# A two-layer decoder trunk on one core: Norm's sum one ff1 tile later, two block jobs behind each turned piece, and another chunk order for k's first tile

## The chip, the cores and the metric

The kernel runs on one core of one Trainium2 chip. The metric is the device time of one execution in microseconds. Engines are called as in the profile: PE is TensorE, DVE is VectorE, ACT is ScalarE, POOL is GpSimd, SP is SyncE, which issues most of the DMAs.

## What is computed

A trunk of two layers over 256 tokens and 2048 channels, in fp32. Cut to what matters here:

```
def squared_relu_mlp(h, w1, w2):            # w1: 2048 x 8192, w2: 8192 x 2048
    z = jax.nn.relu(h @ w1)
    return (z * z) @ w2

def reference(x, mem, ...):
    for i in range(2):
        if i == 1:                           # shared keys and values for layer 1
            sk1, sk2, sv = shared_kv(x, ...) # rms_norm(x, kv_norm) @ w_kv, keys normed and rotated
        u = rms_norm(x, mix_norm[i]) @ w_in[i]
        token_out = pooling mixer (layer 0) or differential attention over sk1, sk2, sv (layer 1)
        mem_out = memory_cross_attention(...)
        x = x + jnp.concatenate([token_out, mem_out], axis=-1) @ w_out[i]
        x = x + squared_relu_mlp(rms_norm(x, ffn_norm[i]), w_ff1[i], w_ff2[i])
    return x
```

`rms_norm(x, g)` is `x * rsqrt(mean(x*x) + 1e-6) * g`.

## The kernel before

**Precision and layout.** Activations lie transposed: 16 chunks of 128 channels by 256 tokens (`resid`). Each fp32 operand is split in two parts of a shorter format: `hi`, a cast on ACT (L199 for weights), and `lo`, the rest, a subtraction on DVE (L202 for weights). A product is hi·hi + hi·lo + lo·hi, with fp32 sums in a PSUM bank. An activation chunk holds both parts side by side, 512 columns. In `a_part` (L472, L474) one matmul of 512 columns does hi weights against both halves, and one of 256 columns does lo weights against the high half. In `wide_step` (L506 to L508) the roles are turned: the activation chunk is loaded as weights and four weight blocks are streamed, 512 columns, for two halves `t` of the tokens, so one chunk is six matmuls and a tile has two banks, `ps[0]` and `ps[1]`.

**The feed.** Weights come in blocks of 128 x 128 in the order of their use. `Feed` loads eight blocks per DMA into one of four `raw` buffers, and splits them up to three pieces of work ahead (`AHEAD`) into rings `hi_ring`, `lo_ring` and some spare places (`zb`, `t_acc`, `t_rowsq`). The host lays the weights out in the order that a dry run of the program has written down.

**The order.** The program is written in the order of TensorE's work. `tick()` counts every four blocks; `at(d, fn)` puts a function `d` ticks later. The framework's planner then sets each engine's order from the program order and its own estimates of costs, so that an instruction of one engine may stand ahead of one that the program names earlier.

**The MLP, `ffn(l, ...)`.** ff1 has 64 tiles of 16 blocks (`up_tile`). Tiles 0 to 2 take banks of the tag "mm" (three), tile 3 and all later ones the one bank of the tag "st" (`bank()`, named `x_bank`). ff2 runs beside ff1 in "block jobs": the 8192 inner channels are taken in 32 pairs of chunks, and a pair's 2 x 2 blocks are multiplied with seven products instead of eight, with sums and differences of weight slabs (DVE L240, L254, and an accumulating DMA from POOL, L163) and of activations (`convert`, DVE L831 to L836, cast L841, low half L845). A slab is four jobs of 6, 3, 6 and 6 matmuls (`product`, L916, L918, L919, into seven banks `p`). There are 60 slabs, 240 jobs. `tiles_at(s)` gives each slab a due time in tiles, and `due(tiles, least)` runs jobs up to that time, at least `least` of them, while more than 12 are left; it is called ahead of each tile with `least=2` and inside it after 4, 8 and 12 blocks. The last 12 jobs run in `down`.

**Norm's sum.** The MLP's input norm is put off: `fx` has the gain but not the factor. `rstd_from("x")` multiplies the running sum of squares `acc` (POOL, L745 and L746 in `add_square`, one pair for each output chunk of the layer before) with ones on TensorE (L531, into a bank of the tag "st" by `stat()`), and turns it into 1/sqrt with three ACT operations (L421, L423, L425) and two on DVE (L368, called from `stt`). It is called in `up_tile` behind tile 0; three ticks later `columns` does the same per token (L540), six ticks later the factor is squared on ACT (L862).

**Turned pieces.** Towards the end of ff1 the left half of ff2's output is complete in token-major rows. `close_left` takes it from the banks, and four pieces are transposed on TensorE (`turn_left`, L1020, into `bank()`, copied out by ACT, L816) ahead of tiles 60 to 63 and added to `resid` on DVE (L1028).

**The end of the MLP and k's first tile.** `down` runs eight down tiles for what is left of ff2 (tiles 0 to 2 in `x_bank`, tiles 3 to 7 in "mm" banks, emptied by DVE L891, added L892) and transposes the other eight chunks (`finish_banks`, L1059, L1060) at ticks between them. Each closed chunk goes into `x_kv` (ACT L450, DVE L368). Then `map_tile` for the keys takes the 16 chunks of `x_kv` as `wide_step`s, into banks of `pair_of_banks`:

```
def pair_of_banks(c, name):
    if c % 2:
        return [pp.tile([P, 512], F32, tag="s", bufs=2, name=name) for _ in range(2)]
    return [mmt(name) for _ in range(2)]     # two of the three "mm" banks
```

Of the kernel before, what the change touches and what calls it, by code (L numbers as in the profile page):

```python
# [19 lines left out]
NK = 16  # L20
# [310 lines left out]
def program(ctx, tc, plan, dry, xT, memT, par, lam, cst, wst, yT):  # L331
    nc = tc.nc
# [15 lines left out]
    def at(d, fn, rank=1):  # L348
        pend.setdefault(now[0] + d, []).append((rank, fn))

    def tick():
        now[0] += 1
        for _, fn in sorted(pend.pop(now[0], []), key=lambda x: x[0]):
            fn()
# [103 lines left out]
    def a_part(ps, w, l, n, ks, xs, first=True, last=True, between=None):  # L458


        ks = list(ks)
        i = 0
        while i < len(ks):
            if between:
                between(i)
            two = []
            for k in ks[i : i + 2 - feed.pos % 2]:
                two.append((i, k % NK, *feed.block((w, l, k, n, 1))))
                feed.used()
                i += 1  # L470
            for c, k, hi, lo in two:
                nc.tensor.matmul(ps, hi, xs[:, k, :], start=first and c == 0, stop=False)  # L472
            for c, k, hi, lo in two:
                nc.tensor.matmul(  # L474
                    ps[:, T : 2 * T], lo, xs[:, k, 0:T], start=False,
                    stop=last and c == len(ks) - 1,
                )
            if feed.pos % 4 == 0:
                tick()
# [10 lines left out]
            if feed.pos % 4 == 0:  # L490
                tick()

    def wide_step(ps, what, xs, k):
        hi, lo = feed.quad(what)
        x = [(xs[:, k, t * P : t * P + P], xs[:, k, T + t * P : T + t * P + P]) for t in range(2)]
        if what[:2] == ("w_mem_kv", 0) and k < 2:

            for t in range(2):
                nc.tensor.matmul(ps[t], x[t][0], hi, start=k == 0, stop=False)
            for t in range(2):  # L500
                nc.tensor.matmul(ps[t], x[t][1], hi, start=False, stop=False)
            for t in range(2):
                nc.tensor.matmul(ps[t], x[t][0], lo, start=False, stop=False)
        else:
            for t in range(2):
                nc.tensor.matmul(ps[t], x[t][1], hi, start=k == 0, stop=False)  # L506
                nc.tensor.matmul(ps[t], x[t][0], hi, start=False, stop=False)  # L507
                nc.tensor.matmul(ps[t], x[t][0], lo, start=False, stop=k == NK - 1)  # L508
        feed.used(4)
        tick()  # L510

# [1 line left out]
        for k in range(NK):  # L513
            wide_step(ps, (w, l, k, c, 4), xs, k)

    def map_tile(ps, w, l, blocks, xs):

        for k in range(NK):
            wide_step(ps, [(w, l, k, n, 1) for n in blocks], xs, k)

    def by_head(row, d):

# [6 lines left out]
    def rstd_from(name):  # L529
        st = stat("st_" + name)  # L530
        nc.tensor.matmul(st, ones_d, acc[name], start=True, stop=True)  # L531
        r = cp.tile([P, T], F32, tag="r_" + name, name="r_" + name)
        rsqrt(r, st)
        return r

    def columns(name, tag="st"):

        st = pp.tile([P, T], F32, tag=tag, bufs=1, name="tc_" + name)
        for i in range(2):
            nc.tensor.matmul(  # L540
                st[:, 2 * i : 2 * i + 2], acc[name][:, i * P : i * P + P], ones_d[:, 0:2],
                start=True, stop=True,
            )
        v = tp.tile([P, 2], F32, tag="m2", bufs=12, name="cv")
        nc.vector.tensor_scalar_add(v, st[:, 0:4].rearrange("p (a b) -> p a b", b=2)[:, :, 0], EPS)
        col = cp.tile([P, 2], F32, tag="c_" + name, name="c_" + name)
        rsqrt_cols(col, v)
        col2 = cp.tile([P, 2], F32, tag="d_" + name, name="d_" + name)
        nc.vector.tensor_mul(col2, col, col)
        return col, col2  # L550
# [218 lines left out]
    def ffn(l, xs, tags, done):  # L769
# [52 lines left out]
        def convert(i):  # L822
            u = staged[:, i % 2, :]
            n = 512 if i == 31 else 1024 if i >= 28 else 896

            def block(b, c=1):
                return u[:, b * P : (b + c) * P]

            def combine():
                twice = block(A21).unsqueeze(1).to_broadcast([P, 2, P])  # L830
                nc.vector.tensor_add(  # L831
                    block(S1, 2).rearrange("p (a c) -> p a c", a=2), twice,
                    block(A22, 2).rearrange("p (a c) -> p a c", a=2),
                )
                nc.vector.tensor_add(block(S2), block(S1), block(A11))
                nc.vector.tensor_add(block(S4), block(A12), block(S2))  # L836
                at(1, lambda: when(lambda: i == 31 or pair_free[i % 5], high))

            def high(a=0, b=n):
                pair_free[i % 5] = False  # L840
                nc.scalar.copy(pair(i)[:, 0, a:b], u[:, a:b])  # L841
                at(1, lambda: low(a, b))

            def low(a, b):
                nc.vector.tensor_sub(  # L845
                    pair(i)[:, 1, a:b], u[:, a:b], pair(i)[:, 0, a:b].bitcast(F32)
                )
                if a == 0:
                    done_pairs.add(i)

            if i < 31:
                return combine()
            assert pair_free[i % 5]
            high(512, 1024)
            at(1, combine)

        def up_tile(i, ps, between=None):
            a_part(ps, "w_ff1", l, i, range(NK), xs, between=between)
            if i == 0:
                r.append(rstd_from("x"))  # L860
                at(3, lambda: r.append(columns("x", "o")[1]))
                at(6, lambda: nc.scalar.activation(r[0], r[0], AF.Square))  # L862
            out = nc.scalar.copy(two_y[:, 1 - i % 2, :], ps)
            if i == 3 and not dry:
                feed.cast_behind = [out.ins.name] * 3
            if i % 2 == 0:
                return
            left, right = two_y[:, :, 0:T], two_y[:, :, T : 2 * T]
            d = 0 if i == 63 else 1

            def add():
                nc.vector.tensor_add(left, left, right)

            at(1, add) if d else add()

            def square():
                assert i < 4 or i // 2 - 2 in done_pairs
                nc.scalar.activation(left, left, AF.Relu)
                u = staged[:, i // 2 % 2, 512:1024].rearrange("p (a c) -> p a c", a=2)
                nc.scalar.activation(u, left, AF.Square)  # L880
                at(1, lambda: convert(i // 2))

            at(1 + d, square)
# [207 lines left out]
        def tiles_at(s):  # L1091

            return early[s] if s < 12 else 20 + (s - 12) * 44 / 46

        def due(tiles, least=0):
            n = 0
            while len(jobs) > 12:
                s, j = jobs[0]
                if tiles_at(s) + j * (tiles_at(s + 1) - tiles_at(s)) / 4 > tiles and n >= least:
                    break  # L1100
                one_job()
                n += 1
# [6 lines left out]
        for i in range(4, 64):  # L1109
            due(i, 2)  # L1110
            if turns:
                turn_left(turns.pop(0))
                due(i, 1)
            up_tile(i, bank(), lambda b, i=i: due(i + b / 16) if b > 0 and b % 4 == 0 else None)
        due(64)
        assert len(jobs) == 12 and not turns
# [30 lines left out]
    xs = sp.tile([P, NK, 512], F32R, tag="S2", name="xs0")  # L1147
# [61 lines left out]
    for i in range(2):  # L1209
        c = slice(2 * i, 2 * i + 2)  # L1210
# [21 lines left out]
    ps = [mmt("mq0"), pp.tile([P, 512], F32, tag="o", bufs=1, name="mq0")]  # L1232
# [12 lines left out]
    for i in range(2):  # L1245
        c = slice(2 * i, 2 * i + 2)
# [110 lines left out]
    x_kv = sp.tile([P, NK, 512], F32R, tag="S2", name="x_kv")  # L1357
# [42 lines left out]
    at(14, lambda: c1.extend(columns("x")))  # L1400
    for c in range(3):
        ps = pair_of_banks(c, "k1")
        map_tile(ps, "w_kv", 0, (2 * c, 2 * c + 1, 6 + 2 * c, 7 + 2 * c), x_kv)
        rows = key_rows(ps, c1, 64)
        rope(rows, ktab)
        for i in range(2):
            at(
                9,
                lambda i=i, c=c, rows=rows: turn_rows(
                    rows, 2 * i, kT[:, 4 * c + 2 * i : 4 * c + 2 * i + 2, :], gcol(G_KN)  # L1410
                ),
            )
    for c in range(3):
        ps = pair_of_banks(c + 1, "v1")
# [8 lines left out]
    ps = pair_of_banks(0, "mk1")  # L1423
    b_tile(ps, "w_mem_kv", 1, 0, mems1)
    mrow1 = key_rows(ps, mem_c, P)
    ps = pair_of_banks(1, "mv1")
# [7 lines left out]
    for t in range(2):  # L1434
        four = "p (h d) -> p h d"
        hi, v4 = mv1[:, t, :].rearrange(four, h=4), ps[t].rearrange(four, h=4)
        split_rows(hi, mv1_lo[:, :, t, :], v4, mem_c[0][:, t : t + 1])
    for i in range(2):
        c = slice(2 * i, 2 * i + 2)
# [114 lines left out]
    for c in range(3):  # L1554
        ps = pair_of_banks(0, "q1")
# [17 lines left out]
    for h in range(4):  # L1573
        ps = mmt("mq1")
        x = ps[:, 0:T]
        if h < 3:
            a_part(ps, "w_in", 1, 12 + h, range(NK), x_mx)
            x = vt("mq_x")
# [102 lines left out]
```

## Time and profile before

| | us |
|---|---|
| median of 3 runs | 2009.33 (2009.01 to 2012.25) |
| profiled execution | 2008.67 |
| its span, first to last instruction | 2006.9 |
| TensorE busy | 1992.0 (99%) |
| VectorE busy | 1731.0 (86%) |
| ScalarE busy | 1456.1 (73%) |
| GpSimd busy | 156.8 (8%) |

The span is what the trace covers; the profiled execution's time is 1.77 us longer. The mean granted clock of TensorE is 0.999 of full speed, and the DMA engines read 418.00 MB, 209 GB/s over the span. A row of the timeline reads: start in us from the span's start, duration in us, engine, line of the kernel, operation, output <- inputs, shapes, how many are merged, and in brackets the idle time before it and what ended it. In such a row of PE with `x2` the duration runs to the end of the second matmul; matmuls overlap, so the distance of their starts is the pace.

### The profile page before, as it was taken

Reading aid. Unit: us, or ns where it says so; the run is one execution under the profiler, and the core shown is the slowest. Engines: PE = TensorE matmul, PEld = TensorE weight load, DVE = VectorE, ACT = ScalarE, POOL = GpSimd, SP = SyncE. Lnnn points to the kernel's source line nnn. Section 1 sums busy time; section 2 is a strip of 40 time slices with the busy share of each in tenths; the row PEclk is TensorE's granted clock in tenths of the full one; section 3 lists DMA queues with packets and bytes.
Section 4 is the critical chain, followed back from the end, with each engine's and each line's share of the span. In section 5 each row is a group of like instructions: output and inputs, shape, how many; then the busy total and the mean of one; then the engine's idle time right before and its main releaser. Section 6 shows DMA issues by size and latency. Waiting matters only on the chain.

```text
span 2006.9 us, 30220 instructions
## 1 busy us (share of the span) xinstructions
PE 1992.0 (99%) x10510; PEld 1700.8 (85%) x10510; DVE 1731.0 (86%) x2574; ACT 1456.1 (73%) x2316; POOL 156.8 (8%) x187
## 2 busy tenths in 40 slices
PE   9999999999999999999999999999999999999998
PEld 8888888888888888888888888888888888888887
DVE  8888778989989899999765698868889999899998
ACT  7765567687786878877665699557777777868875
POOL 0001210000000001000000000320000010000000
PEclk9999999999999999999999999999999999999999
DMA  9555577777778777755565533667777777777773
GB/s 318 173 190 192 183 226 217 226 221 235 226 229 240 222 223 232 225 178 168 181 235 193 179 127 127 201 204 221 225 218 233 229 235 230 222 238 222 231 227 114
DMA packets 145018, 422.09 MB, mean 210 GB/s; under 512 B 16353, under 2 KB 19041, under 8 KB 144865
## 3 DMA queue, kind: packets, MB, share of 16 engines
q1 hardware_dynamic: 127440, 388.69, 58.5%
q0 software_dynamic: 17280, 31.46, 9.3%
q8 instruction: 82, 1.34, 0.3%
q14 instruction: 72, 0.58, 0.1%
q10 hardware_dynamic: 144, 0.01, 0.0%
HBM read 418.00 MB, written 2.10 MB: 209 GB/s over the span
## 4 chain that ended last, share of the span: by engine, by line
PE 97%; DVE 2%; ACT 1%; POOL 0%; issue 0%; ACTq 0%; DVEq 0%
PE x_bank L472 23%; PE x_bank L474 11%; PE p L919 9%; PE p L916 9%; PE p L918 9%; PE wo L472 6%; PE wo L474 3%; PE u L472 2%; PE u L474 1%; PE q L506 1%; PE k L506 1%; PE k L508 1%; PE q L508 1%; PE k L507 1%; PE q L507 1%; PE v L506 1%
## 5 line engine op out<-in xcount | busy, mean ns | idle before, releaser
L202 DVE TENSOR_TENSOR lo_ring<-raw,hi_ring 128x512 fp32r<-128x512 f32 (+1 forms) x632 | 545.1, 870 | 114.9 <-ACT hi_ring L199 106.7
L199 ACT CAST hi_ring<-raw 128x512 fp32r<-128x512 f32 (+1 forms) x632 | 474.8, 756 | 232.5 <-DVE lo_ring L202 57.4
L472 PE MATMUL x_bank<-fx,hi_ring 128*128 128x512 f32 x1440 | 451.0, 394 | 0.8 <-ACT room L816 0.7
L202 DVE TENSOR_TENSOR lo_ring<-slab,hi_ring 128x1024 fp32r<-128x1024 f32 x229 | 279.3, 1223 | 64.8 <-ACT hi_ring L199 63.9
L199 ACT CAST hi_ring<-slab 128x1024 fp32r<-128x1024 f32 x229 | 240.2, 1052 | 128.1 <-PE x_bank L472 62.4
L474 PEld LDWEIGHTS x_bank<-fx,lo_ring 128*128 128x128 f32 x1440 | 270.3, 188 | 62.3 <-DVE lo_ring L202 1.6
L474 PE MATMUL x_bank<-fx,lo_ring 128*128 128x256 f32 x1440 | 283.9, 278 | 0.0
L472 PEld LDWEIGHTS x_bank<-fx,hi_ring 128*128 128x128 f32 x1440 | 236.8, 189 | 21.1 <-ACT room L816 1.7
L163 POOL DMA_DIRECT2D room<-in_w x120 | 103.7, 864 | 1143.1 <-DMA room<-in_w 1117.4
L916 PE MATMUL p<-hi_ring,z 128*128 128x512 f32 x446 | 174.7, 392 | 0.0
L918 PE MATMUL p<-hi_ring,z 128*128 128x512 f32 x446 | 174.4, 391 | 0.0
L919 PE MATMUL p<-lo_ring,z 128*128 128x512 f32 x446 | 172.8, 390 | 0.1
L472 PE MATMUL wo<-cat,hi_ring 128*128 128x512 f32 x512 | 161.9, 397 | 0.3 <-DVE rc L443 0.3
L472 PE MATMUL x_bank<-fx,zb 128*128 128x512 f32 x512 | 160.3, 395 | 0.7 <-ACT room L816 0.7
L474 PEld LDWEIGHTS x_bank<-fx,zb 128*128 128x128 f32 x512 | 96.1, 188 | 22.1 <-DVE zb L202 0.4
L474 PEld LDWEIGHTS wo<-cat,lo_ring 128*128 128x128 f32 x512 | 96.0, 188 | 21.9
L202 DVE TENSOR_TENSOR zb<-slab,zb 128x1024 fp32r<-128x1024 f32 x71 | 86.8, 1223 | 24.3 <-ACT zb L199 24.1
L199 ACT CAST zb<-slab 128x1024 fp32r<-128x1024 f32 x71 | 74.8, 1054 | 39.9 <-PE x_bank L472 23.1
L474 PE MATMUL wo<-cat,lo_ring 128*128 128x256 f32 x512 | 101.6, 279 | 0.0
L474 PE MATMUL x_bank<-fx,zb 128*128 128x256 f32 x512 | 101.0, 278 | 0.0
L919 PEld LDWEIGHTS p<-lo_ring,z 128*128 128x128 f32 x446 | 83.7, 188 | 18.6 <-DVE lo_ring L202 0.5
L916 PEld LDWEIGHTS p<-hi_ring,z 128*128 128x128 f32 x446 | 83.7, 188 | 12.0
(435 smaller groups left out, 4242.9 us busy)
## 6 DMA issues: line engine op xcount, KB each, us to landing
raw<-in_w SPq DMA_DIRECT2D x484, 512.0 KB, 4.1
slab<-in_w SPq DMA_DIRECT2D x120, 512.0 KB, 5.5
room<-in_w SPq DMA_DIRECT2D x180, 256.0 KB, 3.4
room<-in_w POOLq DMA_DIRECT2D x120, 256.0 KB, 6.2
slab<-in_w SPq DMA_DIRECT2D x60, 256.0 KB, 4.8
memraw<-in_mem SPq DMA_DIRECT2D x5, 512.0 KB, 4.4
resid<-in_x SPq DMA_DIRECT2D x8, 256.0 KB, 5.9
out_y<-resid SPq DMA_DIRECT2D x16, 128.0 KB, 1.9
```

What stands on the lines that cost most here:

```text
L163: self.nc.gpsimd.dma_start(self.t1[i], right, accum_op=ALU.add)
L199: self.last_cast = self.nc.scalar.copy(hi, src)
L202: low = self.nc.vector.tensor_sub(lo, src, hi.bitcast(F32))
L472: nc.tensor.matmul(ps, hi, xs[:, k, :], start=first and c == 0, stop=False)
L474: nc.tensor.matmul(ps[:, T : 2 * T], lo, xs[:, k, 0:T], start=False, stop=last and c == len(ks) - 1,)
L506: nc.tensor.matmul(ps[t], x[t][1], hi, start=k == 0, stop=False)
L507: nc.tensor.matmul(ps[t], x[t][0], hi, start=False, stop=False)
L508: nc.tensor.matmul(ps[t], x[t][0], lo, start=False, stop=k == NK - 1)
L916: nc.tensor.matmul(ps, a[1], hi, start=new, stop=False, **again)
L918: nc.tensor.matmul(ps, a[0], hi, start=False, stop=False, **again)
L919: nc.tensor.matmul(ps, a[0], lo, start=False, stop=end, **again)
```

## The change

Three edits. (1) Norm's sum, with the two steps timed from it, is called behind tile 1 of ff1 instead of tile 0, in both layers. (2) Behind each turned piece `due` is called with `least=2` instead of 1. (3) In k's first tile (c = 0) the chunks of `x_kv` are taken in the order 0 to 5, 8 to 11, 6, 12 to 15, 7, and `wide_step` takes its first and last step from that list. The host's layout of the weights follows, since it is written in the order of use; the other two tiles of k keep their order.

```
         def up_tile(i, ps, between=None):
             a_part(ps, "w_ff1", l, i, range(NK), xs, between=between)
-            if i == 0:
+            if i == 1:
                 r.append(rstd_from("x"))
                 at(3, lambda: r.append(columns("x", "o")[1]))
                 at(6, lambda: nc.scalar.activation(r[0], r[0], AF.Square))
...
             if turns:
                 turn_left(turns.pop(0))
-                due(i, 1)
+                due(i, 2)
...
-    def wide_step(ps, what, xs, k):
+    def wide_step(ps, what, xs, k, ks=range(NK)):
...
-                nc.tensor.matmul(ps[t], x[t][1], hi, start=k == 0, stop=False)
+                nc.tensor.matmul(ps[t], x[t][1], hi, start=k == ks[0], stop=False)
...
-                nc.tensor.matmul(ps[t], x[t][0], lo, start=False, stop=k == NK - 1)
+                nc.tensor.matmul(ps[t], x[t][0], lo, start=False, stop=k == ks[-1])
...
-    def map_tile(ps, w, l, blocks, xs):
+    def map_tile(ps, w, l, blocks, xs, ks=range(NK)):
 
-        for k in range(NK):
-            wide_step(ps, [(w, l, k, n, 1) for n in blocks], xs, k)
+        for k in ks:
+            wide_step(ps, [(w, l, k, n, 1) for n in blocks], xs, k, ks)
...
-        map_tile(ps, "w_kv", 0, (2 * c, 2 * c + 1, 6 + 2 * c, 7 + 2 * c), x_kv)
+        ready = [0, 1, 2, 3, 4, 5, 8, 9, 10, 11, 6, 12, 13, 14, 15, 7] if c == 0 else range(NK)
+        map_tile(ps, "w_kv", 0, (2 * c, 2 * c + 1, 6 + 2 * c, 7 + 2 * c), x_kv, ready)
```

## The prediction

> **What bounds the kernel now.** I read the page first, then TensorE's own waits, then the timeline round each wait on TensorE, VectorE, ScalarE and GpSimd, and last the windows for the granted clock.
>
> ```profile
> span 2006.9 us, 30220 instructions
> PE 1992.0 (99%) x10510; PEld 1700.8 (85%) x10510; DVE 1731.0 (86%) x2574; ACT 1456.1 (73%) x2316; POOL 156.8 (8%) x187
> PE 97%; DVE 2%; ACT 1%; POOL 0%; issue 0%; ACTq 0%; DVEq 0%
> ```
>
> TensorE is busy 1992.0 of 2006.9 us and the chain that ended last is TensorE for 97%. The change takes no matmul away, so all that it can win lies in the 14.9 us between busy time and span, and in time at a lower clock. TensorE's waits name nearly all of it:
>
> ```profile
> PE st_x L531 <- POOL acc L746: 4.1, 2, 2.1
> PE k L506 <- DVE room L891: 2.9, 1, 2.9
> PE x_bank L472 <- ACT room L816: 1.4, 2, 0.7
> ```
>
> Columns: total us, times, longest. Each part of the change stands opposite one of these rows: Norm's sum, k's first tile, the turned piece. Together 8.4 us. The question for each is whether the edit removes what the wait waits for.
>
> The pace and the granted clock (eighth column) come from three windows, the first two behind k's wait, the third behind Norm's sum in layer 1:
>
> ```profile
> 930.40:934.00 3.60, 3.58 (x9) 2.88 (x10) 3.27 (x8) 1.83 (x4) 0.00 (x0) 0.54 0.30 90
> 934.00:938.00 4.00, 4.00 (x18) 3.28 (x18) 4.00 (x9) 3.42 (x10) 0.00 (x0) 0.98 0.58 183
> 1335.00:1339.00 4.00, 3.83 (x21) 3.35 (x22) 0.00 (x0) 2.34 (x4) 0.68 (x2) 1.00 1.00 292
> ```
>
> At full clock 18 matmuls of 512 columns start in 4.00 us, 0.22 us each; a block job or a chunk of k, six of them, is 1.33 us.
>
> **Part 1, Norm's sum behind the second ff1 tile.** Layer 0, TensorE, GpSimd, then VectorE:
>
> ```profile
> 256.35 0.39 PE L474 MATMUL ff<-fx,lo_ring 128*128 128x256 f32 x2
> 258.76 0.70 PE L531 MATMUL st_x<-acc,ones_d 128*128 128x256 f32 x2 [2.02 <-POOL acc L746]
> 259.11 0.81 PE L472 MATMUL ff<-fx,hi_ring 128*128 128x512 f32 x2
> 263.48 0.50 PE L540 MATMUL tc_x<-ones_d,acc 128*128 128x2 f32 x4
> 265.32 0.63 PE L472 MATMUL ff<-fx,hi_ring 128*128 128x512 f32 x2
> 270.89 0.63 PE L472 MATMUL x_bank<-fx,hi_ring 128*128 128x512 f32 x2
> 276.46 0.40 PE L916 MATMUL p<-hi_ring,z 128*128 128x512 f32 x1
> ```
>
> ```profile
> 257.11 1.59 POOL L746 TENSOR_TENSOR acc<-acc,psq 128x256 f32<-128x256 f32 x1
> ```
>
> ```profile
> 263.46 0.69 DVE L240 TENSOR_TENSOR slab<-room,slab 128x512 f32<-128x512 f32 x1 [5.33 <-DMA room<-in_w]
> 264.07 0.42 DVE L368 SCALAR_TENSOR_TENSOR rs_t<-st_x,rs_t 128x256 f32<-128x256 f32 x1
> 264.52 0.43 DVE L368 SCALAR_TENSOR_TENSOR r_x<-rs_t,rs_h 128x256 f32<-128x256 f32 x1
> 271.97 1.09 DVE L845 TENSOR_TENSOR z<-stage,z 128x896 fp32r<-128x896 f32 x1
> 274.11 0.69 DVE L202 TENSOR_TENSOR t_rowsq<-room,t_acc 128x512 fp32r<-128x512 f32 x1
> ```
>
> The sum's matmul stands behind the first ff1 tile and needs the last square, which GpSimd ends at 257.11 + 1.59 = 258.70. The tile had issued all it had by about 256.58 (the two 256-column matmuls of the row 256.35 at half of 0.22 us each). One tile lasts 270.89 - 265.32 = 5.57 us, so behind the second tile the sum comes up at about 256.58 + 5.57 = 262.15, 3.4 us after the square is done. The wait is covered. Price of the removal in layer 0: 258.76 - 256.58 = 2.18 us, and some 0.1 us because the restart is slow (0.81 us for the first two matmuls, where the same two take 0.63, is partly that). Layer 1:
>
> ```profile
> 1332.68 0.40 PE L474 MATMUL ff<-fx,lo_ring 128*128 128x256 f32 x2
> 1335.16 0.70 PE L531 MATMUL st_x<-acc,ones_d 128*128 128x256 f32 x2 [2.09 <-POOL acc L746]
> 1352.87 0.40 PE L916 MATMUL p<-hi_ring,z 128*128 128x512 f32 x1
> ```
>
> ```profile
> 1350.34 0.69 DVE L202 TENSOR_TENSOR t_rowsq<-room,t_acc 128x512 fp32r<-128x512 f32 x1
> ```
>
> There 1335.16 - 1332.90 = 2.26 us and the same 0.1. Sum: 4.4 + 0.2 = 4.6 us. The sum's own matmuls are only moved.
>
> What is late next? Three ScalarE operations and two of VectorE (rows 264.07 and 264.52) now come one tile later, the two columns of sums at the third quarter of the third tile, and the square of r_x in the fourth. No DMA and no GpSimd instruction is issued by the moved step, and no order on SP or GpSimd changes by it. VectorE stands at row 263.46 waiting for a transfer. That transfer is not timed by the tiles, so it lands at the same time while TensorE is 2.2 us earlier. From there VectorE has work in its queue to 274.80 (274.11 + 0.69); the first block job, 276.46 now, would start at 274.2. It needs the z low half, done at 271.97 + 1.09 = 273.06: 1.1 us in hand. Job 1 needs the row at 274.11 at its third matmul, 1.33 + 0.44 us after job 0 starts, at 276.0: 1.2 us in hand. Layer 1 is alike: that row ends at 1351.03, 1.84 us ahead of its first job where layer 0 has 1.66. Bound: nothing lost, or up to the 2.2 us of each layer if the rows slide. I take 0.2 us in all.
>
> The fourth tile takes the only bank of the sum (`bank()` and `stat()` share tag "st"). Until now two tiles lay between, now one: from 262.6 to the fourth tile at about 262.6 + 5.57 + 0.36 = 268.5, where 0.36 is what the row 263.48 delays the next matmuls (they start at 263.84). The last reader of the sum is the row 264.07; it follows the row 263.46, over at 264.15, and at worst two low halves that would stand ready there, some 1.2 us each: about 267.0. 1.5 us in hand; cost nothing. Part 1: 4.6 - 0.2 = 4.4 us won.
>
> **Part 2, two jobs behind a turned piece.** Where do the two waits stand? Both at the fourth piece:
>
> ```profile
> 879.63 0.60 PE L1020 MATMUL x_bank<-const,room 128*128 128x128 f32 x4
> 880.27 0.58 ACT L816 COPY room<-x_bank 128x512 f32<-128x512 f32 x1 [0.93 <-PE x_bank L1020]
> 880.90 0.73 PE L472 MATMUL x_bank<-fx,zb 128*128 128x512 f32 x2 [0.68 <-ACT room L816]
> ```
>
> No p matmul stands between piece and tile. The code says why. `due` stops at 12 jobs left, whatever `least` is, and 240 jobs less 12 end with job 3 of slab 56. Tile 60 takes jobs 53.3, 54.0, piece, 54.1; tile 61 takes 54.3, 55.0, piece, 55.1; tile 62 takes 55.3, 56.0, piece, 56.1, and 56.2 within the tile; tile 63 takes 56.3, piece, and nothing is left. After the change 54.2, 55.2 and 56.2 stand behind the first three pieces instead of behind block 12 of the tile, and tile 63 is as before. So the 1.4 us stay. At the first three pieces the one job covers the copy already; piece 0 of layer 0:
>
> ```profile
> 849.07 0.58 ACT L816 COPY room<-x_bank 128x512 f32<-128x512 f32 x1
> 849.75 0.69 PE L472 MATMUL x_bank<-fx,zb 128*128 128x512 f32 x2
> 850.27 1.23 DVE L202 TENSOR_TENSOR lo_ring<-slab,hi_ring 128x1024 fp32r<-128x1024 f32 x1
> ```
>
> The copy is over at 849.65 and the tile starts at 849.75 with no wait. The moved jobs cost their 1.33 us of matmuls in either place. Risk: their low halves must be there about 4 us earlier. 54.2 would ask for its low half two matmuls behind where the tile starts now, at 850.2, and has it at 850.27 + 1.23 = 851.5 in the old order: at worst 1.3 us, at six pieces 8 us. But the change also brings its preparation ahead of the tile's, and the tile's first weights are ready to stand between. I take 0, with 0 to 2.4 us (0.4 at each) for the range.
>
> **Part 3, k's chunks.** TensorE and VectorE at k's start:
>
> ```profile
> 926.03 0.40 PE L506 MATMUL k<-hi_ring,x_kv 128*128 128x512 f32 x1
> 927.07 0.40 PE L507 MATMUL k<-hi_ring,x_kv 128*128 128x512 f32 x1
> 930.42 0.56 PE L506 MATMUL k<-hi_ring,x_kv 128*128 128x512 f32 x1 [2.95 <-DVE room L891]
> ```
>
> ```profile
> 928.36 1.67 DVE L368 SCALAR_TENSOR_TENSOR x_kv<-resid,param,x_kv 128x256 fp32r<-128x256 f32 x4
> 929.95 0.42 DVE L891 TENSOR_TENSOR room<-ff,r_x 128x256 f32<-128x256 f32 x1
> 934.56 0.48 DVE L368 SCALAR_TENSOR_TENSOR x_kv<-resid,param,x_kv 128x256 fp32r<-128x256 f32 x1
> ```
>
> The wait comes after five matmuls, within the first two chunks, and ends with L891: that line empties a bank of a down tile and writes no chunk. Down tiles 3 to 7 turn through the three "mm" banks, so k's two banks are those of tiles 5 and 6. The rows of L891 stand in the order of the tiles; this one is tile 6, held up by the four x_kv splits at 928.36. It is the bank for k's second half of the rows. Both orders begin with chunks 0 to 5, so the change leaves this wait where it is. Chunk 7, the last to close, is there at 935.04; the old order asks for it seven chunks of 1.33 us after 926.03 at the earliest, 935.3, and in fact after the wait and the slow stretch. So the new order has nothing to win behind the wait either: 0, between 0 and the whole 2.95 us. The Trainium skill, "TensorE: Matmul & The Clock Gate", Part 2, states that matmuls stay in program order and only weight loads are pulled ahead; by that k's ready chunks cannot step in for the late bank, and the trace agrees, with nothing issued between 927.07 and 930.42. A reordering queue would have made it 2.95 us less.
>
> The wait has a second price. In 930.40 to 934.00 the granted clock is 0.54 and 9 matmuls take what 18 take in the next 4.00 us: 3.6 - 2.0 = 1.6 us. The idle times of 2.02 and 2.09 us at Norm's sum left the clock at 1.00. So it falls for an idle time of some 3 us, perhaps only if it lies so. k starts 2.3 us earlier after the change, and the 1.6 us may not come back. The Trainium skill, same page, Part 1, states a free-running window of 3413 ns, of which one idle one halves the clock; the trace agrees as far as the slow stretch is about that long, and by that rule the 1.6 us would go or stay by chance.
>
> **Sum.** Profiled execution 2008.67 us (span 2006.9 and 1.77 outside it). Part 1 -4.4, part 2 0, part 3 0: 2004.3 us. The median of the runs, 2009.33, is 0.66 above the profiled one; from it the sum is 2004.9. A measurement of this kernel can tell about 0.2%, 4.0 us: faster is below 2005.3, slower above 2013.4. The forecast lies just beyond the edge.
>
> **Rivals.**
> A, forecast: part 1 alone works, 2004.3 (2003.3 to 2005.6). Chance 0.41.
> B: the same, and the slow stretch behind k's wait does not return: 2004.3 - 1.6 = 2002.7. For it: the lower idle times cost no clock. Against: the 2.95 us stay as they are. 0.25.
> C: the diff does all that it says; k's wait and its slow stretch go too, 2004.3 - 2.95 - 1.6 = 1999.8, with the piece's wait 1998.4. Against: the bank, and the job count. 0.08.
> D: the covers are too thin. VectorE, late by its transfer, holds the first block job, or a low half holds the jobs behind the pieces; 1.0 to 3.5 us come back: 2006.5. For it: VectorE has only 1.1 us in hand. 0.18.
> E, slower: the sum's bank. If the row 264.07 falls in VectorE's queue behind everything that stands there till 274.80, the fourth tile waits from 268.5 to about 275.2, 6.7 us, and such an idle time brings the slow clock with 1.6: 8.3 in each layer, 16.6 - 4.6 = 12 us lost, 2020.7. It costs more than it wins from a read that ends 2.3 us late, behind 270.8. Against: until now the row came right behind the transfer. 0.08.
>
> From these: faster 0.62 (A mostly, B, C), same 0.30 (the rest of A, D), slower 0.08. The range 2001.0 to 2007.8 holds A, B and most of D; C and E lie outside.
>
> **What would show it.** Right: no wait of st_x for acc; the sum's matmul about 5.6 us later than the first tile's end; the x_bank waits for L816 still two of 0.7 us behind the fourth piece; k still waiting about 3 us for L891. Wrong: a wait of x_bank for rs_t or r_x at the fourth tile, of p for z or lo_ring at the first block job or behind a piece, or k's wait gone.

## The result and the profile after

The changed kernel takes 2003.36 us (median of 7 runs, 2001.65 to 2004.7); the kernel before, timed beside it, 2009.33 us (median of 7 runs, 2008.37 to 2012.53). The ratio is 0.9968, with a 95% interval of 0.9956 to 0.9979: 6.0 us, or 0.3%, faster. The profiled execution took 2003.26 us, 5.41 us less than the one of before.

The page of the kernel after: its span, busy times and the shares of the chain that ended last.

```profile
span 2001.5 us, 30206 instructions
PE 1990.5 (99%) x10510; PEld 1699.4 (85%) x10510; DVE 1730.7 (86%) x2574; ACT 1456.2 (73%) x2316; POOL 157.7 (8%) x187
PE 97%; DVE 1%; ACT 1%; issue 0%; DMA 0%; SPq 0%; DVEq 0%; ACTq 0%
```

The span is 5.4 us shorter and TensorE's busy time only 1.5 us: most of what went was idle time. Which idle time it was, TensorE's waits tell (total us, times, longest), from the longest down:

```profile
PE k L506 <- DVE room L891: 2.9, 1, 2.9
PE x_bank L472 <- ACT room L816: 1.4, 2, 0.7
PE warm L413 <- PEq L1655: 0.8, 1, 0.8
PE mk L499 <- DVE mems L1173: 0.7, 1, 0.7
```

The wait of st_x for acc, 4.1 us before, is gone. The first three rows are those of before, to the tenth. The fourth is not in the kernel before, but it lies in the first 9 us, and the loop behind it (mk, L506) starts at 11.1 us in both kernels: it cost nothing. TensorE's timeline at Norm's sum, layer 0, and the fourth tile and first block job of layer 1:

```profile
261.88 0.39 PE L474 MATMUL ff<-fx,lo_ring 128*128 128x256 f32 x2
262.11 0.59 PE L531 MATMUL st_x<-acc,ones_d 128*128 128x256 f32 x2
262.35 0.82 PE L472 MATMUL ff<-fx,hi_ring 128*128 128x512 f32 x2
266.72 0.50 PE L540 MATMUL tc_x<-ones_d,acc 128*128 128x2 f32 x4
268.56 0.63 PE L472 MATMUL x_bank<-fx,hi_ring 128*128 128x512 f32 x2
274.13 0.40 PE L916 MATMUL p<-hi_ring,z 128*128 128x512 f32 x1
...
1342.39 0.63 PE L472 MATMUL x_bank<-fx,hi_ring 128*128 128x512 f32 x2
1347.96 0.40 PE L916 MATMUL p<-hi_ring,z 128*128 128x512 f32 x1
```

No row has a bracket with an idle time. The first block job starts at 274.13 (276.46 before, 2.33 us earlier), in layer 1 at 1347.96 (1352.87 before, 4.91 us earlier). VectorE beside it:

```profile
262.07 0.69 DVE L240 TENSOR_TENSOR slab<-room,slab 128x512 f32<-128x512 f32 x1 [4.00 <-DMA room<-in_w]
266.72 0.43 DVE L368 SCALAR_TENSOR_TENSOR rs_t<-st_x,rs_t 128x256 f32<-128x256 f32 x1 [1.08 <-ACT rs_t L425]
271.59 1.08 DVE L845 TENSOR_TENSOR z<-stage,z 128x896 fp32r<-128x896 f32 x1
```

The sum's bank is read out at 266.72 + 0.43 = 267.15, 1.41 us ahead of the fourth tile; the z low half is done at 271.59 + 1.08 = 272.67, 1.46 us ahead of the first job. TensorE at the first and the fourth turned piece:

```profile
846.00 0.60 PE L1020 MATMUL x_bank<-const,room 128*128 128x128 f32 x4
848.07 0.63 PE L472 MATMUL x_bank<-fx,zb 128*128 128x512 f32 x2
848.53 0.62 PE L919 MATMUL p<-lo_ring,z 128*128 128x512 f32 x2
...
877.21 0.60 PE L1020 MATMUL x_bank<-const,room 128*128 128x128 f32 x4
878.48 0.73 PE L472 MATMUL x_bank<-fx,hi_ring 128*128 128x512 f32 x2 [0.68 <-ACT room L816]
```

Behind the first piece the second job now runs, and the planner's order has the tile's first two matmuls ahead of the two that need the job's low half, with no wait. Behind the fourth piece nothing has changed. TensorE and VectorE at k:

```profile
923.40 0.43 PE L506 MATMUL k<-hi_ring,x_kv 128*128 128x512 f32 x1
924.50 0.39 PE L507 MATMUL k<-hi_ring,x_kv 128*128 128x512 f32 x1
927.83 0.50 PE L506 MATMUL k<-hi_ring,x_kv 128*128 128x512 f32 x1 [2.95 <-DVE room L891]
...
925.78 1.66 DVE L368 SCALAR_TENSOR_TENSOR x_kv<-resid,param,x_kv 128x256 fp32r<-128x256 f32 x4
927.37 0.41 DVE L891 TENSOR_TENSOR room<-ff,r_x 128x256 f32<-128x256 f32 x1
```

k starts 2.63 us earlier, waits in the same place for the same line, and behind it stands the same slow stretch (windows; the eighth column is the granted clock):

```profile
929.00:932.50 3.50, 3.50 (x10) 2.73 (x9) 3.43 (x9) 2.12 (x6) 0.00 (x0) 0.51 0.48 150
932.50:936.00 3.50, 3.50 (x17) 2.90 (x16) 3.50 (x8) 3.50 (x9) 0.00 (x0) 1.00 0.72 219
```

### The profile page after: what moved, and what is told of

Same layout as the page of the kernel before. It is cut to its first block, busy times and chain, and to the rows that moved or that the text cites. A ratio compares the mean times of both kernels' runs of the same rounds, so it can differ in the third digit from the quotient of the medians.

```text
span 2001.5 us, 30206 instructions
## 1 busy us (share of the span) xinstructions
PE 1990.5 (99%) x10510; PEld 1699.4 (85%) x10510; DVE 1730.7 (86%) x2574; ACT 1456.2 (73%) x2316; POOL 157.7 (8%) x187
## 4 chain that ended last, share of the span: by engine, by line
PE 97%; DVE 1%; ACT 1%; issue 0%; DMA 0%; SPq 0%; DVEq 0%; ACTq 0%
PE x_bank L472 23%; PE x_bank L474 11%; PE p L919 9%; PE p L916 9%; PE p L918 9%; PE wo L472 6%; PE wo L474 3%; PE u L472 2%; PE ff L472 1%; PE u L474 1%; PE q L506 1%; PE k L506 1%; PE k L508 1%; PE q L508 1%; PE k L507 1%; PE v L508 1%
## 5 line engine op out<-in xcount | busy, mean ns | idle before, releaser
L202 DVE TENSOR_TENSOR lo_ring<-raw,hi_ring 128x512 fp32r<-128x512 f32 (+1 forms) x631 | 542.9, 868 | 113.4 <-ACT hi_ring L199 104.7
L472 PE MATMUL x_bank<-fx,hi_ring 128*128 128x512 f32 x1424 | 445.8, 394 | 1.4 <-ACT room L816 1.4
L202 DVE TENSOR_TENSOR lo_ring<-slab,hi_ring 128x1024 fp32r<-128x1024 f32 x222 | 270.3, 1221 | 64.4 <-ACT hi_ring L199 63.8
L199 ACT CAST hi_ring<-slab 128x1024 fp32r<-128x1024 f32 x222 | 232.6, 1052 | 125.7 <-PE x_bank L472 58.6
L472 PE MATMUL x_bank<-fx,zb 128*128 128x512 f32 x528 | 165.0, 394 | 0.0
L474 PEld LDWEIGHTS x_bank<-fx,zb 128*128 128x128 f32 x528 | 99.2, 188 | 22.4
L202 DVE TENSOR_TENSOR zb<-slab,zb 128x1024 fp32r<-128x1024 f32 x78 | 95.1, 1219 | 24.0 <-ACT zb L199 23.6
L199 ACT CAST zb<-slab 128x1024 fp32r<-128x1024 f32 x78 | 82.2, 1053 | 41.2 <-PE x_bank L472 27.8
L472 PEld LDWEIGHTS x_bank<-fx,zb 128*128 128x128 f32 x528 | 87.5, 189 | 7.5
```

Source lines behind the costliest of these rows:

```text
L199: self.last_cast = self.nc.scalar.copy(hi, src)
L202: low = self.nc.vector.tensor_sub(lo, src, hi.bitcast(F32))
L474: nc.tensor.matmul(ps[:, T : 2 * T], lo, xs[:, k, 0:T], start=False, stop=last and c == len(ks) - 1,)
```

## The experiments

Theory ahead of the runs: the move of Norm's sum is the whole gain; the other two parts move work that waits for nothing they touch. Rivals: the jobs or the chunk order bring a share of their own, or k's wait hangs on something other than the bank.

**One part at a time.** The kernel before with the sum's move alone, `e1_norm`:

```
-            if i == 0:
+            if i == 1:
                 rstd_from("x")
```

> The kernel before with Norm's sum moved alone. My theory (only this part works): 4.6 us faster than before, about 2003.9 against 2008.67 in a profiled execution, and the same as the whole change within 0.8 us; the two waits of st_x for acc are gone, k's wait of 2.9 us and the two of 0.7 us at x_bank stay. Rival (the other two parts bring the 0.8 us by which the whole change went beyond 4.6): 0.8 us or more slower than the whole change.

Measured: 2003.92 us (6 runs) against 2010.57 (22 runs of the kernel before), ratio 0.9968 (0.9957 to 0.998), the ratio of the whole change. (That the two medians are so near is in part the clock, as the table below shows.) The k and piece waits stand at 2.9 and 1.4 us as ever. One thing is new: in layer 1 the fourth tile waits for the sum's bank. VectorE and ScalarE, then TensorE:

```profile
1339.31 0.69 DVE L240 TENSOR_TENSOR slab<-room,slab 128x512 f32<-128x512 f32 x1 [6.59 <-DMA room<-in_w]
1342.19 0.68 DVE L872 TENSOR_TENSOR room<-room 128x512 f32<-128x512 f32 x1
1342.91 0.63 ACT L878 ACTIVATE room<-room 128x512 f32<-128x512 f32 x1 [3.77 <-DVE room L872]
1343.45 0.40 ACT L425 ACTIVATE rs_t<-rs_h 128x256 f32<-128x256 f32 x1
1343.96 0.42 DVE L368 SCALAR_TENSOR_TENSOR rs_t<-st_x,rs_t 128x256 f32<-128x256 f32 x1 [1.08 <-ACT rs_t L425]
...
1344.44 0.73 PE L472 MATMUL x_bank<-fx,hi_ring 128*128 128x512 f32 x2 [0.45 <-DVE rs_t L368]
```

This is the wait that rival E names, at 0.45 us instead of 6.7. The way to it leads over ScalarE: the last of the sum's three operations there (L425) stands behind L878, L878 waits for VectorE's L872, and L872 stands in VectorE's queue behind L240 and two low halves. From the start of L240 to that of rs_t it is 4.65 us here and in both layers of the whole change. In this execution the transfer that L240 waits for landed about 2 us later against the sum's matmul than in the profiled execution of the whole change. So the 1.4 us in hand there can be used up by one late transfer.

The second job alone, `e2_jobs`:

```
-                due(i, 1)
+                due(i, 2)
```

> The kernel before with two block jobs behind each turned piece alone. My theory: no change, 0 +- 0.5 us against before, since no job is left behind the fourth piece where the two waits of 0.7 us are; both waits stay. Rival 1 (the diff's aim): both gone, 1.4 us faster. Rival 2 (the moved jobs want their low halves too early): waits of p for lo_ring or zb behind the first three pieces, up to 0.4 us each, 2.4 us slower.

The chunk order alone, with the list in `wide_step` as in the change, `e3_order`:

```
-        map_tile(ps, "w_kv", 0, (2 * c, 2 * c + 1, 6 + 2 * c, 7 + 2 * c), x_kv)
+        ready = [0, 1, 2, 3, 4, 5, 8, 9, 10, 11, 6, 12, 13, 14, 15, 7] if c == 0 else range(NK)
+        map_tile(ps, "w_kv", 0, (2 * c, 2 * c + 1, 6 + 2 * c, 7 + 2 * c), x_kv, ready)
```

> The kernel before with the new chunk order of k's first tile alone. My theory: 0 +- 0.5 us, since k's wait is for a bank; the wait of k L506 for DVE L891 stays at 2.9 us and the half clock behind it too. Rival (the wait is for the chunks that close last): the wait gone, 2.9 to 4.5 us faster.

Measured: `e2_jobs` 2009.43 us (11 runs), ratio 0.9996 (0.9987 to 1.0005); `e3_order` 2010.01 us (11 runs), ratio 0.9997 (0.9988 to 1.0006). By their medians, neither can be told from no change. Both profiles show the three waits of before at their old sizes, to 0.1 us, and no new one where the change touches anything.

The timelines tell the two apart, in stretches that hold no slow clock. From layer 0's first block job to k's start it is 649.57 us in before, 649.54 in `e1_norm`, 649.73 in `e3_order`; with the second job 649.28 in `e2_jobs` and 649.27 in after. From the end of VectorE's last operation to the end of the span, where the last outputs are written, it is 3.6 to 3.7 us in those three and 3.2 in these two; in layer 1, from the first job to the last matmul, the five lie within 0.1 us of each other. So the second job does bring something, about 0.3 + 0.4 to 0.5 us, some 0.8 in all. The 0.3 us lie between the fourth turned piece and k, not at the two waits; why a gain comes there and in the last outputs, no run shows.

What these two profiles also show is the clock. Windows behind Norm's sum in `e2_jobs` (both layers), then the same window as the first in the kernel before, then the window behind k's wait in `e3_order`:

```profile
259.50:262.90 3.40, 3.40 (x11) 2.85 (x11) 0.00 (x0) 1.90 (x4) 0.00 (x0) 0.50 1.02 267
1338.10:1341.50 3.40, 3.40 (x13) 2.92 (x12) 0.00 (x0) 2.04 (x4) 0.89 (x1) 0.50 0.97 289
```

```profile
259.50:262.90 3.40, 3.40 (x21) 2.97 (x20) 0.00 (x0) 2.35 (x4) 0.89 (x1) 1.00 0.99 274
```

```profile
930.40:934.00 3.60, 3.47 (x15) 2.84 (x16) 3.53 (x9) 2.59 (x6) 0.00 (x0) 1.00 0.21 71
```

The idle time ahead of the sum in `e2_jobs` is 2.0 us, as before, and here it is followed by 3.4 us at clock 0.50, 11 matmuls where the other execution had 21. In `e3_order` k waited its 2.95 us and lost nothing behind it. Whether an idle time of 2 or 3 us is followed by half clock thus differs from execution to execution of what is the same code there. The spread of the runs goes with the clock; sorted by their mean granted clock, mean us (runs):

| kernel | 1.000 | 0.999 | 0.998 | 0.997 |
|---|---|---|---|---|
| before | | 2008.95 (11) | 2010.47 (26) | 2012.14 (10) |
| after | 2001.65 (1) | 2003.43 (4) | 2004.65 (2) | |
| e1_norm | 2003.12 (3) | 2005.07 (2) | 2005.94 (1) | |
| e2_jobs | | 2008.53 (4) | 2009.96 (5) | 2011.50 (2) |
| e3_order | 2007.54 (1) | 2009.01 (4) | 2010.23 (3) | 2012.59 (3) |
| e4_banks | 2002.68 (4) | 2003.36 (1) | | |
| e5_turns | 2002.39 (2) | 2003.49 (2) | 2004.22 (1) | |
| e6_fourth | | 2001.96 (3) | 2002.99 (2) | |
| e7_third | | 2011.07 (2) | 2012.09 (4) | 2013.00 (5) |
| e8_all | 2000.98 (2) | 2002.77 (3) | | |
| e9_spread | | 2000.91 (5) | | |
| e10_square | | 2003.91 (4) | 2005.22 (2) | |

A thousandth of mean clock is about 1.5 us; one stretch of 3.4 us at half clock is 1.7/2007, or 0.85 thousandths. A stretch can also be twice as long. Behind k's wait in `e1_norm`:

```profile
927.30:934.10 6.80, 6.04 (x14) 4.79 (x15) 6.24 (x14) 2.83 (x6) 0.00 (x0) 0.50 0.30 96
```

At equal clock (0.999) after is 5.5 us faster than before, and `e1_norm` 1.3 to 1.6 us slower than after (three columns). Against the runs of before that were timed beside them, `e1_norm` is 4.2 to 4.6 us faster at equal clock and `e2_jobs` 0.6 to 1.0. A column is as wide as 1.5 us and holds few runs, so this is weak by itself; it agrees with the timelines in giving the second job part of the gain.

**The sum one tile later still,** `e7_third`, the change with the sum behind the third tile:

```
-            if i == 1:
+            if i == 2:
```

> The changed kernel with Norm's sum behind the third ff1 tile instead of the second. Nothing is left out. Theory (the fourth tile takes the sum's only bank, so the move has a far end): the fourth tile waits for rs_t, the sum's last reader on VectorE, 2 to 4 us in each layer, 4 to 8 us slower than the whole change and more where the clock falls. Rival (the tile's bank is no bound): same as the whole change within 0.5 us.

Measured: 2012.36 us (11 runs) against 2010.36 (15), ratio 1.001 (1.0001 to 1.0019): the gain is gone and 2 us with it. The wait stands elsewhere than expected. TensorE, then VectorE:

```profile
271.19 0.50 PE L916 MATMUL p<-hi_ring,z 128*128 128x512 f32 x1 [2.13 <-DVE z L845]
272.94 0.68 PE L472 MATMUL x_bank<-fx,hi_ring 128*128 128x512 f32 x2
...
270.05 1.09 DVE L845 TENSOR_TENSOR z<-stage,z 128x896 fp32r<-128x896 f32 x1
272.41 0.42 DVE L368 SCALAR_TENSOR_TENSOR rs_t<-st_x,rs_t 128x256 f32<-128x256 f32 x1
```

With the sum later in the only bank, the planner put the first block jobs ahead of the fourth tile. These then wait for z, 4.7 us in both layers together, which the fourth tile had covered. A tile of distance from the sum to the fourth tile is needed; the second tile is the last place that keeps it.

**What made the sum late,** `e10_square`, the kernel before with the sum in its old place, but the last chunk's square on ScalarE and its addition on VectorE instead of GpSimd:

```
         if act:
             nc.scalar.activation(sq, src, AF.Square)
+            nc.vector.tensor_add(acc[key], acc[key], sq)
+            return
...
-            add_square("x", resid[:, n, :], n == 0)
+            add_square("x", resid[:, n, :], n == 0, n == NK - 1)
```

> The kernel before, with Norm's sum left behind the first ff1 tile, but the last chunk's square taken by ScalarE and added by VectorE instead of both on GpSimd. Nothing is left out. Theory (the sum waited for GpSimd's queue, where a DMA's issue of 1 us and two slow operations of 0.9 and 1.6 us stand one behind the other): the waits of st_x fall from 4.1 to below 0.5 us, 4 to 5 us faster than before at equal clock and about 6 us in the median, like the moved sum. Rival (what comes behind the sum needs that time, so only the place of the sum helps): a new wait of 1.5 us or more in each layer's first tiles, and less than 2 us gained.

Measured: 2004.33 us (6 runs) against 2009.97 (10), ratio 0.997 (0.9959 to 0.9982). TensorE in `e10_square`, and GpSimd in the kernel before, ahead of the row of 257.11 that stands in the prediction:

```profile
256.43 0.59 PE L531 MATMUL st_x<-acc,ones_d 128*128 128x256 f32 x2
```

```profile
255.37 1.01 POOL L163 DMA_DIRECT2D room<-in_w  x1 [7.20 <-PE ff L474]
256.12 0.92 POOL L745 TENSOR_TENSOR psq<-resid 128x256 f32<-128x256 f32 x1
```

The sum stands behind the first tile as before and waits for nothing. So the wait was GpSimd's: in the kernel before, the issue of a transfer stands ahead of the last square, then come 0.92 and 1.59 us for two operations. Covering the wait and removing what is waited for come out alike.

**What k waits for.** `e4_banks`, the change with k's first tile in the two "s" banks, which are free by then, and the users after it swapped:

```
-        ps = pair_of_banks(c, "k1")
+        ps = pair_of_banks(c + 1, "k1")
...
-        ps = pair_of_banks(c + 1, "v1")
+        ps = pair_of_banks(c, "v1")
...
-    ps = pair_of_banks(0, "mk1")
+    ps = pair_of_banks(1, "mk1")
...
-    ps = pair_of_banks(1, "mv1")
+    ps = pair_of_banks(0, "mv1")
...
-        ps = pair_of_banks(0, "q1")
+        ps = pair_of_banks(1 - min(c, 1), "q1")
```

> The changed kernel, with k's first tile in the two banks of the tag s instead of two of the tag mm, and the pairs of the tiles behind it exchanged alike. Nothing is left out. My theory (k waits for the bank of down tile 6): the wait of 2.9 us is gone and the half clock behind it with it, 4.5 us faster than the whole change, about 1998.8 in a profiled execution; if k then overtakes its chunks, a wait of x_kv below 1 us. Rival (k waits for chunks): the wait stays or returns at another chunk with 2 us or more.

Measured: 2002.65 us (5 runs) against 2010.57, ratio 0.9962 (0.995 to 0.9975). The wait for L891 is gone, and one of the same size stands five matmuls further on. TensorE, then VectorE:

```profile
928.82 0.73 PE L508 MATMUL k<-lo_ring,x_kv 128*128 128x512 f32 x2 [2.92 <-DVE lo_ring L202]
...
926.62 0.42 DVE L891 TENSOR_TENSOR room<-ff,r_x 128x256 f32<-128x256 f32 x1
926.96 0.87 DVE L368 SCALAR_TENSOR_TENSOR x_kv<-resid,param,x_kv 128x256 fp32r<-128x256 f32 x2
928.08 1.29 DVE L202 TENSOR_TENSOR lo_ring<-raw,hi_ring 128x512 fp32r<-128x512 f32 x2
```

I had expected 4.5 us less than the whole change; at clock 1.000 the four runs of `e4_banks` take no less than the one of after. The bank was what k waited for by name, and VectorE's queue is what bounds it. Behind the bank's copy the queue holds the low halves of k's next weights, and they come no earlier (L202 at 927.70 in the profile after, at 928.08 here). No slow stretch follows the wait in this execution, but a new wait of 1.4 us stands further on, of k's per-token sums (tc_x, L540) for VectorE's acc (L756).

`e5_turns`, the change with the last two of the four turns, two chunks each, two ticks later, so that their additions and splits stand further back in that queue:

```
-                at(8 + h // 2 * 2, lambda h=h: turn(h))
+                at(8 + h // 2 * 4, lambda h=h: turn(h))
```

> The changed kernel with the last two of the four transposed pieces of the down stage two ticks later (tick 12 instead of 10), so that their two adds and four chunk splits stand behind down tile 6's eviction and behind k's first two weight halves in VectorE's queue. Nothing is left out. Theory now (VectorE's queue ahead of k is the bound, for the bank and for the weights' low halves alike): k's wait of 2.9 us falls below 1 us, the half clock behind it goes, 3 to 4.5 us faster than the whole change, unless the sums of squares come late behind it (tc_x, up to 1.4 us). Rival (k's wait is the bank's or the weights' alone, whatever the queue): a wait of 2 us or more stays at k.

Measured: 2002.42 us (5 runs) against 2010.36, ratio 0.9965 (0.9952 to 0.9979). I had expected less than 1 us of wait to be left; it was this, again for a low half:

```profile
931.67 1.04 PE L508 MATMUL k<-lo_ring,x_kv 128*128 128x512 f32 x2 [2.19 <-DVE lo_ring L202]
```

The work that moved back in VectorE's queue met k further on.

**The fourth piece,** `e6_fourth`, the change with one job of the last twelve put behind the fourth piece:

```
                 due(i, 2)
+                if i == 63:
+                    one_job()
...
-        assert len(jobs) == 12 and not turns
+        assert len(jobs) == 11 and not turns
...
-                for _ in range((8, 2, 2, 0, 0, 0, 0, 0)[n]):
+                for _ in range((7, 2, 2, 0, 0, 0, 0, 0)[n]):
```

> The changed kernel with one of the 12 jobs that are held back run behind the fourth turned piece (7 + 2 + 2 stay for later). Nothing is left out. Theory (the two waits of x_bank for L816 stand where no job is left): both gone, 1.4 us faster than the whole change, about 2001.9 in a profiled execution. Rival (the copy's time comes back, since the last stage then has one job less of cover): the wait moves to the first down tile, 0 +- 0.5 us.

Measured: 2002.15 us (5 runs) against 2010.36, ratio 0.9963 (0.995 to 0.9975). TensorE:

```profile
877.23 0.60 PE L1020 MATMUL x_bank<-const,room 128*128 128x128 f32 x4
877.59 0.47 PE L916 MATMUL p<-hi_ring,zb 128*128 128x512 f32 x1
```

The job follows the piece and both waits of 0.7 us are gone. At equal clock (0.999) it is 1.5 us below the change, the 1.4 us that they were worth; against the change's median, 1.2 us is within the intervals. So part 2's idea holds, at the one piece which part 2 does not reach.

**All together.** `e8_all` is the change with `e5_turns`, `e6_fourth` and the per-token sums for k one tick later (`at(15, ...)` for `at(14, ...)`). `e9_spread` is that with the last two of the four turns at ticks 14 and 16 instead of both at 12:

```
-                at(8 + h // 2 * 4, lambda h=h: turn(h))
+                at((8, 8, 14, 16)[h], lambda h=h: turn(h))
```

> The changed kernel with the later transposed pieces, the job behind the fourth turned piece, and the token sums for k one tick later (15 instead of 14). Nothing is left out. Theory: k's wait, the x_bank waits and tc_x's wait are gone together, 4 to 6 us faster than the whole change, about 1998.5, with the granted clock at 1.000. Rival (VectorE gives it back in k's stage): less than 2 us faster.

> As the run with all three edits, but the last two transposed pieces of the down stage at ticks 14 and 16, within k's first tile, instead of both at 12. Nothing is left out. Theory (VectorE has more queued ahead of k's low halves than TensorE leaves it time; whichever stands in front of them, k waits until it is through): with the two adds and four splits behind the low halves of k's first chunks the wait of 2.2 us falls below 1 us, 2 us faster than that run where the clock is full, about 1998.7. Rival (the work only moves to where it is waited for again): a wait of 1.5 us or more at a later chunk or at tc_x, and no gain.

Measured: `e8_all` 2002.61 us (5 runs, 2000.93 to 2003.0) against 2010.36, ratio 0.9961 (0.9949 to 0.9974), with 2.2 us of k's wait left: not the 4 to 6 us below the whole change that I had expected. `e9_spread` 2000.95 us (5 runs, 2000.24 to 2001.47) against 2009.97, ratio 0.9954 (0.994 to 0.9968). It has the lowest median of all, 2.4 us below the change's; the two were timed in different sets and the intervals of their ratios overlap. I had expected its k wait to fall below 1 us; 2.0 us are left. TensorE, ScalarE, VectorE:

```profile
937.53 0.73 PE L508 MATMUL k<-lo_ring,x_kv 128*128 128x512 f32 x2 [1.99 <-DVE lo_ring L202]
...
934.07 1.14 ACT L199 CAST hi_ring<-raw 128x512 fp32r<-128x512 f32 x2 [1.79 <-PE k L507]
935.12 0.90 ACT L450 ACTIVATE x_kv<-resid,param 128x256 fp32r<-128x256 f32 x2
...
935.65 0.88 DVE L368 SCALAR_TENSOR_TENSOR x_kv<-resid,param,x_kv 128x256 fp32r<-128x256 f32 x2 [1.82 <-ACT x_kv L450]
```

Read backwards: k waits for a low half; VectorE had stood still 1.82 us for the high half of the last chunks; ScalarE had that behind two weight casts, and those waited 1.79 us for k's own matmuls. Spread this far, the work is no longer bound by how much VectorE has to do, but by one order on ScalarE. A version with that order changed was not tried.

## Why the prediction was right, and where a size was off

**Part 1, predicted 4.6 us gross and 4.4 net: measured 4.7.** Layer 0 gave 2.33 us (2.18 + 0.1 predicted). Layer 1 gave 4.91 - 2.55 = 2.36, where 2.55 is how much earlier layer 1's first ff1 tile starts (1327.34 before, 1324.79 after). The working hit its own marks: the sum at 262.15 predicted and 262.11 in the trace, the fourth tile 268.5 and 268.56, the first job 274.2 and 274.13. The covers came out near their forecast as well, 1.5 us for the bank and 1.41 seen, 1.1 for z and 1.46 seen, but that was luck: two errors cancelled. The transfer for L240 does not land at a fixed time; VectorE goes on at 263.46 in one execution and at 262.07 in the other. And the sum's last reader does not follow it directly, as the working has it, but over L872, L878 and L425, 4.65 us behind L240's start, where it was 264.07 - 263.46 = 0.61 before. The z low half starts 9.52 us behind it instead of 8.51. Before, L425 followed the operation ahead of it at once; the working had no term for its new place in ScalarE's order. With its own 263.46 for the transfer, the bank would have been read out at 263.46 + 4.65 + 0.42 = 268.53, with the fourth tile at 268.56, and z done at 274.06, with the first job at 274.13: nothing in hand in either place. The 0.2 us that I took off were not lost here, but `e1_norm` shows where they can be, in a fourth tile 0.45 us late. In the fourteen layers of the seven profiles with the sum behind the second tile this is the only wait of that kind.

**Part 2, predicted 0: right about the waits, and some 0.8 us short.** No job is left for the fourth piece, where both waits stand (878.48), and the low half at the first piece is covered by the tile's own matmuls (848.07 ahead of 848.53). `e6_fourth` removes the waits by supplying the job. But the forecast looked at these waits alone and had no term for a gain elsewhere; the timelines show 0.3 us ahead of k and 0.4 to 0.5 in the last outputs with the second job, within the -2.6 to +1.0 us that `e2_jobs` allows by its interval.

**Part 3, predicted 0: right in size, and the reason only half of it.** k did wait for the bank of L891, and the chunk order did nothing (`e3_order`, -2.4 to +1.2 us). But I treated the bank as the cause. `e4_banks` took it away and got the same 2.9 us from the next row of the same queue. Rival C's price for k's wait was thus not to be had by the other banks of `e4_banks`, nor by the order of k's chunks.

**The clock, wrong.** The prediction reasoned that the idle times of 2.02 and 2.09 us had left the clock at 1.00, "so it falls for an idle time of some 3 us". That was one execution. `e2_jobs` shows both of these idle times followed by 3.4 us at 0.50, `e3_order` a 2.95 us wait followed by 1.00. So the two waits that part 1 removes cost not only their idle time but, in a share of executions, some 1.7 us each, and the term should have read 4.6 plus a part of 3.4. What it measured: 5.97 us between medians, against 4.7 for part 1 and 0.8 for part 2 in the timelines, which leaves 0.5 us. The clocks point the same way: their mean over the 47 runs of the kernel before in the table is 0.9980, over after's 7 it is 0.9989; at 1.5 us for a thousandth that is 1.3 us, though these 47 runs were not timed beside after's. For the same reason rival B was no separate case: k's slow stretch came back in the profiled execution, and the run at mean clock 1.000, which took 2001.65 us, has no room for a whole one. Its price of 1.6 us was near: from k's start to layer 1's first ff1 tile it is 401.31 us in before and 400.02 in `e3_order`, where the stretch is absent, 1.3 us less.

The Trainium skill, "TensorE: Matmul & The Clock Gate", Part 1, gives a free-running window of 3413 ns and a drop to half clock after at least one idle window of about 3.4 us. The length of the stretches agrees, 3.4 us or twice that, and that they come in some runs and not in others fits a window that runs free; the idle time that it takes does not agree: 2.0 us was enough in `e2_jobs`.

**What stays open.** The two profiled executions differ by 5.41 us with one slow stretch in each. 4.69 are part 1. About 0.2 came between layer 0's first job (2.33 earlier) and layer 1's first tile (2.55), and about 0.5 lies behind the last matmul (2002.06 before, 1997.13 after, 4.93 earlier), in the last outputs. `e2_jobs` shows that both come with the second job; by which mechanism stays open. In `e7_third` 5.1 us of new waits (4.7 for z, 0.4 for a bank) stand against 7.6 us lost at equal clock (2011.07 less 2003.43); the rest was not traced.

## What to carry to other kernels

When you move a short chain of work, look where each engine's new order puts every link of it; the thinnest cover here hung on one ScalarE operation that had come to stand behind another. Price a wait on a saturated TensorE by its idle time plus a share of the slow clock that may follow it, and take that share from several executions: one profile can show a wait with or without it. Before you free the resource that a wait names, read what stands behind its releaser in the order of the same engine; if the next thing that is needed is queued there, the wait only changes its name. A job moved to cover a wait must be counted at the very place where the wait stands.

## What the runs showed of the hardware

An idle time of 2.0 us on TensorE was followed by 3.4 us at clock 0.50 in one execution and by full clock in another, and an idle time of 2.95 us likewise. Such a stretch lasted 3.4 us or twice that (6.8 us behind k's wait in `e1_norm`), and stood at up to three places in a profiled execution. The runs of the kernel before spread from 2008.4 to 2013.1 us with it, by about 1.5 us for a thousandth of mean granted clock. On GpSimd an addition of 128x256 took 0.72 to 1.61 us where VectorE took 0.42 for one of that shape.
